# Fewer 64-slot experts, fewer of them fetched before the routing is known, and the embedding's weights fetched with them

## The chip, the core and the metric

The kernel runs on one core of a Trainium2 chip, in one launch. The metric is the time of that launch on the device in microseconds (us). Five engines work beside each other: TensorE multiplies matrices, VectorE and ScalarE do elementwise work and move results out of the accumulators, GpSimd does a little, and SyncE only issues DMA transfers, in the order in which they stand in its program.

## The reference

Two layers of a decoder trunk on 256 tokens of width 1024, all in 32-bit floats. Each layer mixes tokens (two kinds of attention, gates, an output projection), normalises, and then runs a mixture of experts plus a small per-layer embedding, and normalises again. The change touches the second half of a layer:

```python
def hierarchical_moe(x, w_rg, b_rg, w_re, b_re, w_g, w_u, w_d):
    ...
    g_val, g_idx = lax.top_k(g_prob, 1)          # one of 4 groups
    ...
    e_val, e_idx = lax.top_k(e_prob, TOP_K_IN_GROUP)   # 2 of its 8 experts
    ...
    for g in range(N_GROUPS):
        hg = jax.nn.silu(jnp.einsum('nd,edf->nef', xt, w_g[g])) * jnp.einsum('nd,edf->nef', xt, w_u[g])
        y = y + jnp.einsum('nef,efd->nd', hg * comb[:, g, :, None].astype(hg.dtype), w_d[g])
    return y.reshape(B, S, D)
...
ple = jax.nn.sigmoid(x @ w_ple_gate[i]) * (p[i] @ w_ple[i])
x = layer_norm(ALPHA * x + ffn + ple, ln2_g[i], ln2_b[i])
```

So 256 tokens are spread over 32 experts, two experts for each token: 512 token places in all. Every expert has 3 MB of weights (gate, up and down, each 1024 by 256).

## The kernel before

**Weights and places.** All big weights come from HBM in blocks of 512 KB, one DMA each. An expert is six blocks: four for gate and up (j = 0 to 3) and two for down (j = 4, 5). SBUF holds an arena of 47 places (`Arena`, `places=47`); a place holds one block, or one tile of activations of that size. `Held` takes a place and `free` gives it back. A load takes the place that has been free longest, and its DMA waits until the last user of that place is done. Which load gets which place is fixed when the program is built.

**Slots and groups.** An expert computes on a fixed number of token slots. `NBIG` experts have 64 slots, the others 32. TensorE takes 128 rows at a time, so a group is either two experts with 64 slots (a **pair**, 12 blocks) or four experts with 32 (a **four**, 24 blocks). `groups` lists them (`npair` pairs, then fours) and `order` says in which order they run. In this text group 0 is the one that runs first. Inside a group the work on TensorE is cut in strips of 32 rows, so a pair and a four issue the same number of instructions of the same size.

**Fixed and ranked experts.** The first `NFIX` experts are experts 0, 1, 2, ... by number. Their weights need no routing, so they are fetched while the attention half still runs, as places come free (`for gi in range(len(groups))` ... `fetch(r, j)`). The other experts are ranked by how many tokens they got; the fullest take the remaining 64-slot ranks. Their numbers land in `ids`, SyncE reads each of them (`value_load`, line 1034) and only then issues that expert's six DMAs (line 1040).

**One turn of the loop over groups.** TensorE's order is written by hand (`manual_schedule`): `front(gi+1)` multiplies the gathered tokens by gate and up; `back(gi)` multiplies the hidden activations by down; then the tokens of group gi+2 are gathered with a one-hot matrix, the hidden activations of gi+1 are transposed, the outputs of gi are scattered back into the accumulators (`combine`), `embeds(gi)` may add a piece of the embedding, and the scatter matrix of gi+2 is made (`ways_of`). `front` frees its blocks two k-steps at a time, `back` frees its blocks at its end.

**Embedding.** It is cut in four quarters (`Embed(q)`): two blocks each, and one more for every two quarters. Quarter 0 is always fetched early. `nemb` says how many further quarters are fetched before the routing is known; the others are fetched when their turn comes. `e0`, `e1`, `early` and `lastat` say after which group a quarter's half (`run(t)`, one half of the tokens) is computed.

**A check for overflow.** After `front` of group 4 (`ifat=3`) all engines branch on whether an expert got more tokens than it has slots (line 1191). Only then `leftover` runs a slow loop over all experts.

**The end of a layer.** `wide(2, l)` and `wide(3, l)` load the second normalisation's scale and shift (line 382) on SyncE's queue, between the second and third of the last group's eight down blocks. In layer 0 the first weights of layer 1 follow.

Of the kernel before, what the change touches and what calls it, by code (L numbers as in the profile page):

```python
# [41 lines left out]
FAR = 1000.0  # L42


NFIX = 6
NBIG = 12


SEC = ["iq", "sq", "sk", "sv", "dq", "dk", "dv", "ga0", "ga1", "gb0", "gb1"]
# [30 lines left out]

@with_exitstack
def tile_hybrid_trunk(ctx: ExitStack, tc: tile.TileContext, x_in, xT_in, pT_in, pos_in, ws, wik, wrt, lnv,
                      brt, lamv, sublnv, out, places=47, t2b=4, young=4, gsb=1, hTb=1, silb=2, nring=5, early=(4, 5, 6), nahead=4, apart=8, npre=36, wA=1, wB=1, wC=1, wD=1, wE=3, inorder=2, e0=2, e1=2,  nearly_=0, peng_=1, ifat=3, im=0, df=0, dh=15, nol=0, diag=1, rpool='0000', lastemb=1, lastat=6, pre_if=(4,5), npair=6, fh=False, fg=0, order=(0,1,2,6,3,7,4,8,5,9,10), engs=None, nemb=1, nwarm=9, nfine=2, nah=4, o1=False, o2=False, o3=True, o4=True, order2=True, pa=2, pb=7, f1=True):
    nc = tc.nc
    V, A, G = nc.vector, nc.scalar, nc.gpsimd

# [20 lines left out]
    def in_turn():  # L107

        return tc.issue_after(PE.last.ins)
# [14 lines left out]
    def bank():  # L124
        return ps.tile([P, 512], F32, tag="mm", bufs=4, name=nm("mm"))
# [128 lines left out]
    def constants():  # L254
# [14 lines left out]
        G.iota(kbon, pattern=[[-1, NE]], base=NE - 1, channel_multiplier=0, allow_small_or_imprecise_dtypes=True)  # L269
        V.tensor_scalar(kbon[:, :NFIX], kbon[:, :NFIX], 1.0e6, None, op0=OP.add)  # L270
        G.iota(kid[:, 0:1], pattern=[[0, 1]], base=0, channel_multiplier=1, allow_small_or_imprecise_dtypes=True)
        V.tensor_scalar(kid[:, 1:2], kid[:, 0:1], float(NFIX), 1.0e6, op0=OP.is_lt, op1=OP.mult)
        V.tensor_tensor(kid[:, 1:2], kid[:, 1:2], kid[:, 0:1], op=OP.subtract)
# [179 lines left out]
    for l in range(DEPTH):  # L453
# [414 lines left out]
        def places_of(b, mask, cols):  # L868

            n = cols.stop - cols.start  # L870
            PE.matmul(b[:, 0:n], trib, mask[:, 0, :], start=True, stop=True)
            PE.matmul(b[:, n:2 * n], onesb, mask[:, 0, :], start=True, stop=False)
            PE.matmul(b[:, n:2 * n], trib, mask[:, 1, :], start=False, stop=True)
            V.scalar_tensor_tensor(posm[:, :, cols], mask, -FAR, b[:, :2 * n].rearrange("p (t e) -> p t e", t=TT),
                                   op0=OP.mult, op1=OP.add)


        groups = [[(r, 2, 64)] for r in range(0, 2 * npair, 2)]
        small = NBIG
        for r in range(2 * npair, NBIG):  # L880
            n = min(2, NE - small)
# [42 lines left out]
        def marks_of(gi):  # L924

            gs = wt([P, TT, P], F32, "gs", gsb)
            c = 0
            for r, n, w in groups[gi]:
                marked[0] = V.tensor_tensor(gs[:, :, c:c + n * w].rearrange("p t (e s) -> p t e s", e=n),
                                            iom[:, None, None, :w].to_broadcast([P, TT, n, w]),  # L930
                                            posm[:, :, r:r + n, None].to_broadcast([P, TT, n, w]), op=OP.is_equal)
                c += n * w
            return gs
# [17 lines left out]
        places = bank()  # L951
# [5 lines left out]
        with in_turn():  # L957
            places_of(places, mkf[:, :, :NFIX], slice(0, NFIX))
        gs = marks_of(0)
        with tc.issue_after(marked[0].ins):  # L960
# [24 lines left out]
            V.tensor_scalar(perm, iom[:NE, :NE], FAR, kcol[:, 2:3], op0=OP.add, op1=OP.is_equal)  # L985
            V.tensor_copy(cw[:, :, :NFIX], cbf[:, :, :NFIX])
        with in_turn():
# [8 lines left out]
        cmi = ids[:, NE:]  # L996
        V.tensor_scalar(ids[:, :NFIX], iom[0:1, :NFIX], FAR, None, op0=OP.add)
        V.tensor_copy(ids[:, NFIX:NE], b[0:1, 2 * NE + NFIX:3 * NE])
        over = cut(NE, rows=1)
        for c, n in (slice(0, NBIG), 64.0), (slice(NBIG, NE), 32.0):  # L1000
            V.tensor_scalar(over[:, c], b[0:1, 3 * NE + c.start:3 * NE + c.stop], n, None, op0=OP.subtract)
# [185 lines left out]
        def leftover(most):  # L1187
            def onward(cols, n):
                V.tensor_scalar(posm[:, :, cols], posm[:, :, cols], float(n), None, op0=OP.add)

            with tc.If(most > 0, preferred_fallthrough_block=False):
                onward(slice(0, NBIG), -64)
                onward(slice(NBIG, NE), -32)
                with tc.For_i(0, 2, 1):
                    with tc.For_i(0, NE, 1) as r:
                        rest(r)
                    onward(slice(0, NE), -P)
                onward(slice(0, NBIG), 64 + 2 * P)
                onward(slice(NBIG, NE), 32 + 2 * P)
# [138 lines left out]
```

## Time and profile before

| | us |
|---|---|
| median of 3 runs | 966.4 (963.85 to 969.9) |
| the profiled execution | 968.06 |
| its span, first to last instruction | 966.5 |
| TensorE busy | 911.4 (94% of the span) |
| VectorE busy | 427.8 (44%) |
| ScalarE busy | 347.7 (36%) |

The profile is of one execution. Each layer has two halves: attention and projections (about 0 to 220 us and 470 to 697 us) and experts (about 228 to 471 us and 704 to 953 us). HBM gave 278.70 MB over the span, 289 GB/s on average. "Busy" on TensorE says that a multiplication was in flight, not that the array was full.

### The profile page before, as it was taken

How to read it: one execution, taken by the hardware profiler on the slowest of the kernel's cores; microseconds unless marked ns; L12 is line 12 of the kernel's file. 1: busy time of each engine (PE TensorE's matmuls, PEld its weight loads, DVE VectorE, ACT ScalarE, POOL GpSimd, SP SyncE). 2: the span in 40 equal slices, each digit the busy share in tenths (PEclk: the TensorE clock that was granted, in tenths of full speed). 3: DMA queues.
4: the chain of work that ended last, by engine and by line, in shares of the span. 5: the costliest groups of instructions: out<-in, count | busy, mean ns of one | idle time of the engine just before them, and what ended most of it. 6: DMA issues, size and time to landing. Idle time of an engine off the chain costs nothing. (4 is left out here: it accounts for less than half of the span.)

```text
span 966.5 us, 15937 instructions
## 1 busy us (share of the span) xinstructions
PE 911.4 (94%) x5761; PEld 605.7 (63%) x5761; DVE 427.8 (44%) x1068; ACT 347.7 (36%) x704; POOL 33.3 (3%) x37
## 2 busy tenths in 40 slices
PE   8999999999998988999799999999999989888994
PEld 5877777785545466544488777787754646456441
DVE  6796566873121211122468864778622121211123
ACT  6557586522111111112346667765121111111120
POOL 0000000100000000000400000001000000000000
PEclk9999999999999999999999999999999999999998
DMA  8994335767899999795997243456869999979933
GB/s 298 408 417 161 125 110 179 261 244 284 320 360 415 388 417 376 310 416 234 397 418 306 88 131 131 139 196 235 305 215 372 378 409 415 399 299 408 370 144 145
DMA packets 79013, 280.86 MB, mean 291 GB/s; under 512 B 9160, under 2 KB 9928, under 8 KB 78928
## 3 DMA queue, kind: packets, MB, share of 16 engines
q1 hardware_dynamic: 78784, 279.78, 76.0%
q8 instruction: 47, 0.77, 0.3%
q14 instruction: 38, 0.31, 0.1%
q10 hardware_dynamic: 144, 0.00, 0.0%
HBM read 278.70 MB, written 1.05 MB: 289 GB/s over the span
## 5 line engine op out<-in xcount | busy, mean ns | idle before, releaser
L92 PE MATMUL acc<-a,a 128*128 128x512 f32 x1440 | 353.2, 399 | 2.1 <-ACT a L208 1.3
L92 PEld LDWEIGHTS acc<-a,a 128*128 128x128 f32 x1440 | 266.0, 189 | 65.1 <-issue 3.2
L92 PE MATMUL mm<-a,a 128*32 128x512 f32 (+5 forms) x1776 | 235.1, 537 | 0.0
L208 ACT ACTIVATE a<-a 128x512 fp32r<-128x512 f32 (+1 forms) x247 | 150.6, 631 | 99.9 <-PE acc L92 69.0
L209 DVE TENSOR_TENSOR a<-a,a 128x512 fp32r<-128x512 f32 (+1 forms) x239 | 161.0, 695 | 50.0 <-ACT a L208 48.6
L92 PEld LDWEIGHTS mm<-a,a 128*32 128x32 f32 (+3 forms) x1776 | 110.7, 132 | 101.4 <-issue 91.1
L92 PE MATMUL mm<-a,hT 128*32 128x512 f32 x704 | 92.2, 604 | 9.0 <-DMA a<-ws 5.0
L92 PEld LDWEIGHTS mm<-gs,a 128*128 128x128 f32 x704 | 80.4, 192 | 17.2 <-PE mm L92 11.7
L92 PE MATMUL mm<-gs,a 128*128 128x128 f32 x704 | 84.7, 278 | 0.0
L1050 ACT ACTIVATE sil<-mm 128x256 f32<-128x256 f32 x22 | 8.4, 383 | 183.2 <-PE mm L92 165.9
L92 PEld LDWEIGHTS mm<-a,hT 128*32 128x32 f32 x704 | 24.3, 111 | 71.5 <-issue 56.5
L1051 DVE SCALAR_TENSOR_TENSOR sil<-sil,wsl,mm 128x256 f32<-128x256 f32 x22 | 10.6, 481 | 131.4 <-ACT sil L1050 131.2
L209 DVE TENSOR_TENSOR t<-mm,t 128x512 fp32r<-128x512 f32 x44 | 30.4, 692 | 68.7 <-ACT t L208 68.7
L208 ACT ACTIVATE t<-mm 128x512 fp32r<-128x512 f32 x44 | 26.3, 597 | 79.0 <-PE mm L92 79.0
L763 DVE TENSOR_TENSOR sil<-sil,mm 128x256 f32<-128x256 f32 x16 | 6.7, 420 | 107.4 <-ACT sil L762 107.4
L92 PE MATMUL acc<-t,sT 128*128 128x512 f32 x176 | 48.8, 413 | 0.0
L906 ACT ACTIVATE a<-mm 128x512 f32<-128x512 f32 x40 | 23.9, 598 | 50.1 <-PE mm L92 50.1
L919 DVE CAST sT<-mm 128x256 fp32r<-128x256 f32 x22 | 9.3, 425 | 69.1 <-PE mm L92 69.1
L92 PEld LDWEIGHTS acc<-t,sT 128*128 128x128 f32 x176 | 31.4, 190 | 9.0 <-issue 2.5
L762 ACT ACTIVATE sil<-mm 128x256 f32<-128x256 f32 x16 | 6.1, 383 | 79.6 <-PE mm L92 79.6
L92 PE MATMUL acc<-t,identr 128*128 128x256 f32 x32 | 12.4, 388 | 21.8 <-ACT t L208 20.6
L548 ACT ACTIVATE t<-mm,mx 128x128 f32<-128x128 f32 (+1 forms) x64 | 26.0, 421 | 10.7 <-DVE mx L545 10.7
(197 smaller groups left out, 648.1 us busy)
## 6 DMA issues: line engine op xcount, KB each, us to landing
a<-ws SPq DMA_DIRECT2D x523, 512.0 KB, 8.4
a<-x_in SPq DMA_DIRECT2D x2, 512.0 KB
out<-a SPq DMA_DIRECT2D x4, 256.0 KB, 2.7
a<-xT_in SPq DMA_DIRECT2D x3, 256.0 KB
a<-wik SPq DMA_DIRECT2D x2, 288.0 KB, 7.6
a<-ws SPq DMA_DIRECT2D x2, 256.0 KB, 4.2
pT<-pT_in SPq DMA_DIRECT2D x2, 256.0 KB
a<-wrt SPq DMA_DIRECT2D x2, 144.0 KB, 2.8
```

Source lines behind the costliest of these rows:

```text
L92: self.last = nc.tensor.matmul(*a, **k)
L208: copied[0] = A.activation(hi, src, AF.Copy)
L209: copied[1] = eng.tensor_tensor(lo, src, hi, op=OP.subtract)
L548: A.activation(e[:, i * nk:(i + 1) * nk], b[:, i * nk:(i + 1) * nk], AF.Exp, bias=mx[:, i:i + 1], accum_out=sums[i])
L762: A.activation(g, b[:, :256], AF.Sigmoid)
L763: V.tensor_tensor(g, g, b[:, 256:], op=OP.mult)
L906: A.activation(xg, b.rearrange("p (k s) -> p k s", k=4), AF.Copy)
L919: V.tensor_copy(sT, b[:, :2 * P].rearrange("p (t q) -> p t q", t=TT))
L1050: A.activation(sil, gu[:, :FE], AF.Sigmoid)
L1051: V.scalar_tensor_tensor(sil, sil, wsl, gu[:, :FE], op0=OP.mult, op1=OP.mult)
```

## The change

```diff
-NFIX = 6
-NBIG = 12
+NFIX = 4
+NBIG = 8
...
-... early=(4, 5, 6) ... lastat=6 ... npair=6 ... order=(0,1,2,6,3,7,4,8,5,9,10) ... nemb=1 ...
+... early=(3, 4, 5) ... lastat=5 ... npair=4 ... order=(0,1,2,4,3,5,6,7,8,9) ... nemb=3 ...
```

Eight experts instead of twelve have 64 slots, and 24 instead of 20 have 32. Before there were six pairs and five fours; now there are four pairs and six fours, ten groups instead of eleven. In run order (P a pair, F a four) it was P P P F P F P F P F F and is now P P P F P F F F F F. Four experts instead of six are fetched before the routing is known (24 blocks instead of 36), and three quarters of the embedding instead of one (beside quarter 0): seven blocks instead of two. Quarters 1, 2 and 3 are computed after groups 3, 4 and 5 instead of 4, 5 and 6. All other settings stay, the 47 places too.

SyncE's queue in layer 0, where the fetches that need no routing end and the ranked ones begin (`a_...` is a place's tile, `ws` the weights, line 1040 an expert's block, line 164 an embedding's). Before:

```order
L1040 DMA a_2301<-ws 128x1024
L1040 DMA a_2303<-ws 128x1024
L1040 DMA a_2305<-ws 128x1024
L164 DMA a_2311<-ws 128x1024
L1034 TENSOR_LOAD ids_2224
L1034 ISA x2
L1040 ISA
L1040 DMA a_2661<-ws 128x1024
```

Now:

```order
L1040 DMA a_2283<-ws 128x1024
L164 DMA a_2287<-ws 128x1024
L164 DMA a_2289<-ws 128x1024
L164 DMA a_2291<-ws 128x1024
L164 DMA a_2293<-ws 128x1024
L164 DMA a_2295<-ws 128x1024
L164 DMA a_2297<-ws 128x1024
L1034 TENSOR_LOAD ids_2224
L1034 ISA x2
L1040 ISA
L1040 DMA a_2530<-ws 128x1024
```

The embedding's blocks now stand ahead of the first read of `ids`, and the expert blocks ahead of it are fewer.

TensorE in layer 0 after the branch, from the end of group 3's `combine` to the start of `front` of group 5 (`sT` scatters, `gs` gathers, `identr` is the identity, the last rows are `front`'s). Before:

```order
L92 MATMUL acc_2075<-t_603_3136,sT_2637 128x512
L95 MATMUL mm_3176<-identr,gs_3139 128x128 x2
L92 MATMUL mm_3176<-cw_2177,gs_3139 128x4 x2
L92 MATMUL mm_3258<-a_3199,a_3141 32x512
L92 MATMUL mm_3258<-a_3210,a_3141 32x512
```

Now:

```order
L92 MATMUL acc_2075<-t_608_3164,sT_2657 128x512
L92 MATMUL mm_3203<-a_2285,a_2069 128x256 x4
L92 MATMUL mm_3203<-a_2287,a_2070 128x256 x4
L92 MATMUL mm_3203<-a_2082,pT_1485 128x256 x2
L92 MATMUL acc_2072<-t_617_3217,identr 128x256 x2
L92 MATMUL mm_3222<-a_2285,a_2069 128x256 x4
L92 MATMUL mm_3222<-a_2287,a_2070 128x256 x4
L92 MATMUL mm_3222<-a_2082,pT_1485 128x256 x2
L92 MATMUL acc_2074<-t_620_3236,identr 128x256 x2
L95 MATMUL mm_3242<-identr,gs_3167 128x128 x2
L92 MATMUL mm_3242<-cw_2177,gs_3167 128x4 x2
L92 MATMUL mm_3324<-a_3265,a_3169 32x512
```

The embedding's quarter 1 (both halves of the tokens) has moved one group earlier, between `combine` of group 3 and `front` of group 5.

## Rows read from the trace of the kernel before

**Rows 1.** The page: busy time of each engine; TensorE and DMA in 40 slices.

```profile
PE 911.4 (94%) x5761; PEld 605.7 (63%) x5761; DVE 427.8 (44%) x1068; ACT 347.7 (36%) x704; POOL 33.3 (3%) x37
...
PE   8999999999998988999799999999999989888994
...
DMA  8994335767899999795997243456869999979933
```

**Rows 2.** Timeline of TensorE, one group of layer 0: start us, us, instructions.

```profile
261.38 7.07 PE L92 MATMUL mm<-a,a 128*32 128x512 f32 x64
268.27 3.62 PE L92 MATMUL mm<-a,hT 128*32 128x512 f32 x32
271.82 3.84 PE L92 MATMUL mm<-gs,a 128*128 128x128 f32 x32
...
275.63 2.10 PE L92 MATMUL acc<-t,sT 128*128 128x512 f32 x8
...
278.23 7.07 PE L92 MATMUL mm<-a,a 128*32 128x512 f32 x64
```

**Rows 3.** Waits on DMA, 228 to 470 us: us in total, times, longest.

```profile
PEld mm L92 <- DMA a<-ws: 8.7, 10, 2.3
...
PE mm L92 <- DMA a<-ws: 2.6, 5, 1.4
```

**Rows 4.** Timeline of TensorE, the last two groups of layer 0.

```profile
446.33 7.07 PE L92 MATMUL mm<-a,a 128*32 128x512 f32 x64
453.22 3.62 PE L92 MATMUL mm<-a,hT 128*32 128x512 f32 x32
...
464.12 1.05 PE L92 MATMUL mm<-a,hT 128*32 128x512 f32 x2 [1.41 <-DMA a<-ws]
...
468.04 2.76 PE L92 MATMUL mm<-a,hT 128*32 128x512 f32 x18 [0.24 <-DMA a<-ws]
```

**Rows 5.** The same, layer 1.

```profile
935.52 3.62 PE L92 MATMUL mm<-a,hT 128*32 128x512 f32 x32
...
952.89 2.22 PE L92 MATMUL acc<-t,sT 128*128 128x512 f32 x8
```

**Rows 6.** Timeline of SyncE's queue around the first ranked fetch, layer 0.

```profile
216.66 0.33 SPq L164 DMA_DIRECT2D a<-ws  x1
228.44 10.98 SPq L1040 DMA_DIRECT2D a<-ws  x9
```

**Rows 7.** The same, layer 1.

```profile
704.52 4.81 SPq L1040 DMA_DIRECT2D a<-ws  x5
```

**Rows 8.** Timeline of SyncE's queue at the end of layer 0.

```profile
436.61 2.88 SPq L1040 DMA_DIRECT2D a<-ws  x3
456.04 0.59 SPq L382 DMA_DIRECT2D a<-lnv  x2
456.85 3.07 SPq L1040 DMA_DIRECT2D a<-ws  x6
```

**Rows 9.** Line 1040's fetches, 228 to 460 us: count; time from issue to landing.

```profile
L1040 SPq DMA_DIRECT2D a<-ws x156: 332/333/1205, 228.4 to 459.6; - x156
...
DMA to landing us min/median/max: 3.3/8.4/10.9
```

**Rows 10.** Stretches: busy us (x) by engine, then granted clock, DMA share, GB/s.

```profile
244.00:248.00 4.00, 4.00 (x39) 1.59 (x41) 1.07 (x4) 0.60 (x1) 0.00 (x0) 1.00 0.29 73
384.00:392.00 8.00, 6.55 (x40) 2.73 (x43) 2.22 (x8) 0.80 (x2) 0.00 (x0) 0.79 0.38 126
400.00:440.00 40.00, 38.55 (x311) 21.86 (x309) 7.86 (x20) 6.76 (x14) 0.00 (x0) 1.00 1.03 416
448.00:457.00 9.00, 9.00 (x87) 2.70 (x79) 1.60 (x3) 0.99 (x3) 0.00 (x0) 1.00 0.02 8
900.00:920.00 20.00, 20.00 (x180) 9.84 (x176) 4.28 (x12) 3.43 (x7) 0.00 (x0) 1.00 0.99 395
```

**Rows 11.** Timeline of TensorE: one embedding quarter, first and following instructions.

```profile
343.90 3.61 PE L92 MATMUL mm<-a,a 128*128 128x256 f32 x16
...
356.98 0.38 PE L95 MATMUL mm<-identr,gs 128*128 128x128 f32 x2
```

**Rows 12.** Timeline of TensorE around the overflow branch of layer 0, and later.

```profile
316.03 5.34 PE L92 MATMUL mm<-a,hT 128*32 128x512 f32 x32 [2.09 <-DVEq L1191]
...
327.71 7.07 PE L92 MATMUL mm<-a,a 128*32 128x512 f32 x64
...
387.56 8.77 PE L92 MATMUL mm<-a,a 128*32 128x512 f32 x64
```

More of the change, by code (lines that the diff above doesn't have):

```diff
@@ L82, in tile_hybrid_trunk @@
 def tile_hybrid_trunk(ctx: ExitStack, tc: tile.TileContext, x_in, xT_in, pT_in, pos_in, ws, wik, wrt, lnv,
-                      brt, lamv, sublnv, out, places=47, t2b=4, young=4, gsb=1, hTb=1, silb=2, nring=5, early=(4, 5, 6), nahead=4, apart=8, npre=36, wA=1, wB=1, wC=1, wD=1, wE=3, inorder=2, e0=2, e1=2,  nearly_=0, peng_=1, ifat=3, im=0, df=0, dh=15, nol=0, diag=1, rpool='0000', lastemb=1, lastat=6, pre_if=(4,5), npair=6, fh=False, fg=0, order=(0,1,2,6,3,7,4,8,5,9,10), engs=None, nemb=1, nwarm=9, nfine=2, nah=4, o1=False, o2=False, o3=True, o4=True, order2=True, pa=2, pb=7, f1=True):
+                      brt, lamv, sublnv, out, places=47, t2b=4, young=4, gsb=1, hTb=1, silb=2, nring=5, early=(3, 4, 5), nahead=4, apart=8, npre=36, wA=1, wB=1, wC=1, wD=1, wE=3, inorder=2, e0=2, e1=2,  nearly_=0, peng_=1, ifat=3, im=0, df=0, dh=15, nol=0, diag=1, rpool='0000', lastemb=1, lastat=5, pre_if=(4,5), npair=4, fh=False, fg=0, order=(0,1,2,4,3,5,6,7,8,9), engs=None, nemb=3, nwarm=9, nfine=2, nah=4, o1=False, o2=False, o3=True, o4=True, order2=True, pa=2, pb=7, f1=True):
     nc = tc.nc
```

## The prediction

> **What bounds the kernel now.** The page comes first. TensorE is busy for 94% of the span, and in the slices of the expert halves TensorE and DMA both read 9 [rows 1], so the page alone can't say which of them sets the pace there. The timeline of TensorE can. In the expert half it is a clockwork: `front` of a group starts at 261.38 and that of the next at 278.23, a period of 16.85 us, with no wait written in between [rows 2]. The waits view agrees: from 228 to 470 us TensorE and its weight loader waited for weight blocks 11.3 us in all [rows 3], and the timeline of the layer's end shows where, namely in `back` of the last group, whose blocks land one after another until 468.04 [rows 4]. The queue's own timeline says why. SyncE issued nothing between 439.5 and 456.04, when the two loads of line 382 at last got their places; six blocks stood behind them [rows 8]. Over 448 to 457 us DMA moved 8 GB/s, against 416 over 400 to 440 us [rows 10]. So TensorE sets the pace of the expert half up to the last group, DMA is kept a limited distance ahead by the 47 places, and a tail follows that the queue sets: 470.80 less 456.84, the end of the next-to-last group's `back`, or 14.0 us [rows 4], and 13.75 in layer 1 (952.89 less 939.14) [rows 5].
>
> **The change part by part.** *One group less.* A pair and a four have the same instructions, so what goes is one period: 16.85 us in each layer, 33.7 in all, as long as TensorE remains the bound. VectorE and ScalarE lose the same group's work; they were at 44% and 36% [rows 1] and give nothing further.
>
> *The embedding* keeps its instructions. One quarter takes TensorE 13.08 us (356.98 less 343.90) [rows 11] wherever it stands. That it runs one group earlier costs nothing by itself, but it decides when places come free (below).
>
> *Fewer blocks ahead of the routing.* Before, 156 expert blocks [rows 9] and five of the embedding's quarters 2 and 3 came behind the first read of `ids`; now 168 expert blocks do and none of the embedding's. A block takes 1.26 us of the queue (524,288 bytes at 416 GB/s [rows 10]), so seven more are 8.8 us more to move in each layer after 228.44, when the first ranked fetch is issued [rows 6]. The queue stood idle ahead of that moment already (its last fetch was issued at 216.66) and will be idle longer, at no cost. What covers the 8.8 us is that TensorE was the bound; whether the cover holds has to be counted.
>
> *Places.* When the numbers are known, 47 places hold 24 fixed blocks, 10 of the embedding, 4 of x and its transpose and 1 of gathered tokens; 8 are free. (Before it was 36, 5, 4, 1: one free. The queue then waited for TensorE to free more, the stretch at 73 GB/s from 244 to 248 us [rows 10]; that stop goes.) Up to the end of `back` of group 3, TensorE frees 48 blocks by the fronts of groups 0 to 4, 20 by the backs of groups 0 to 3 and 2 of the embedding's quarter 0. So 78 blocks can be issued up to 321.4 us, when that `back` ends (316.03 plus 5.34 [rows 12]). At 1.26 us each, 3.3 us after the first issue [rows 9] and with two short stops of 1 us, the 78th lands at about 331. Then the queue stops: quarter 1 now stands ahead of `front` of group 5, which begins not at 327.71 [rows 12] but 13.1 later. Quarter 1's own three blocks come free at about 336, the front's from 342.5 on, and a new block lands 3.3 us after its issue. That is a stop of some 7 us and one of 3, and one of 1 ahead of group 6. My estimate of all stops is 13 us. The bounds are 0 (no place is ever short) and 16: what the queue lost in the same stretch before, 155 blocks issued between 228.44 and 439.5 where 195 us would do. I take 13, near the upper one, because the stretches at 73 and 126 GB/s [rows 10] show that such stops are real.
>
> *Five fours in a row.* A four needs 24 blocks, 30.2 us of the queue, against TensorE's 16.85 us; a pair needs 15.1. In the last five groups TensorE catches up with the queue. The block that decides is number 160, the last one of `back` of group 8, the next-to-last group; the two loads of line 382 and the last six blocks are issued only after it, as before, so the tail stays at 14 us. In layer 0 it lands at 228.44 + 3.3 + 159 x 1.26 + 13 = 445.1, and the 18 instructions behind it take 2.8 us [rows 4], so this `back` ends at 447.9. TensorE alone would end it at 456.84 less 16.85 = 440.0. The later one counts: 447.9 instead of 456.84, a gain of 8.9 us, with 7.9 us of the removed period lost to a new wait for weights. In layer 1 the count starts at 704.52 [rows 7] and gives 923.9; TensorE alone would give 939.14 less 16.85 = 922.3 [rows 5]. The gain is 15.2. Layer 1 does better because it computes the last half quarter of the embedding (6.5 us) inside the loop and not after it, which gives the queue that much more time.
>
> *The clock.* After the 2.09 us wait at the overflow branch, 32 instructions took 5.34 us instead of 3.62 [rows 2, 12], and once later 64 took 8.77 instead of 7.07; the granted clock of 384 to 392 us was 0.79 [rows 10], a mixture of the two levels, 2.4 and 1.2 GHz. Such a fall costs 1.7 us. The new waits could add one in each layer; while TensorE waits for blocks a slower array costs nothing, so the bounds are 0 and 3.4 us for both layers, and I take 0.
>
> The sum is 8.9 + 15.2 = 24.1 us. From the profiled execution's 968.06 us this gives 944.0; that execution was 1.7 us above the median, so against 966.4 it is 942.3. I predict **942 us**.
>
> **The rivals.** *TensorE remains the bound throughout.* If the stops are short (5 us or less in layer 0, 11 in layer 1), both layers keep the whole 16.85: 966.4 less 33.7 = 932.7 us. For it: TensorE waited for nothing before the last group. Against it: the count above.
>
> *The queue is slower than I take it.* The bound would be the same, with a larger price of a block. The lowest rate in a stretch in which DMA was nearly full (0.99) is 395 GB/s [rows 10], 1.327 us for a block; 159 blocks are then 10.7 us later in each layer and the gain shrinks to 24.1 less 21.4, that is 964 us. Halfway, at 405 GB/s, it is 953, which I take for this case. For it: the rows differ by 5%. Against it: the 395 holds moments in which places were short. The Trainium skill ("DMA: Bandwidth & Descriptors", Specifications) speaks against the change more strongly: it puts what HBM gives one core at about 358 GB/s, by which a block would take 1.46 us and the whole, an estimate from that figure, would be near 1,000 us. This trace disagrees, with 416 GB/s over 40 us.
>
> *Stops as long as before, now where they count.* The queue is strictly in order, and places are assigned when the program is built; one block whose place is freed late holds up all behind it. Before, layer 0's queue lost 16 us up to 439.5 and 16.5 more at line 382 [rows 8], and TensorE hardly noticed, because it came later than the blocks. If a stop of the second kind falls ahead of block 160 now, the stops are 33 us instead of 13: both layers end 20 us later than forecast, which makes 24.1 us gained into 15.9 lost, 982 us. The change turns into a loss from about 25 us of stops on average (22 in layer 0, 28 in layer 1). For it: each of the last five groups asks for twice the blocks of a pair. Against it: the two loads of line 382 still stand behind block 162.
>
> *The change doesn't do what it says.* With 32 slots for 24 experts a crowded one would overflow, and `leftover` would stream all experts again: at least 64 x 6 blocks x 1.26 = 484 us in a layer. The reference's routing of its own inputs gives at most 23 tokens (layer 0) and 28 (layer 1) to an expert with 32 slots and at most 45 to one with 64. That ten groups are built, the program's order shows.
>
> **How the numbers follow.** Forecast 0.61; TensorE as the bound 0.12; a slower queue 0.17; longer stops 0.09; overflow 0.01. About 1%, or 9.7 us, is what a measurement of this kernel can tell from no change. Faster by more than that are the forecast, the first rival and 0.12 of the second: 0.85. Within 1% is the rest of the second, 0.05; slower are the last two, 0.10. The range runs from the first rival's 932 to 955: it holds the forecast (stops of 16 us give 948, one fall of the clock in each layer 3.4 more), the first rival and about half of the second, together 0.81.
>
> **What would show it.** In the profile of the changed kernel: ten `front` rows in each layer with a period of 16.85 us up to group 8 where no embedding stands between; stretches of low GB/s near 331 to 341 us; TensorE waiting for blocks in `front` of group 9 and above all `back` of group 8, some 8 us in layer 0 and under 2 in layer 1; then 14 us from that `back` to the end of the experts; the end of layer 1's experts moved from 953 to about 929 us. I am wrong if `front` of groups 5 to 8 waits for blocks, if the last blocks arrive well after 458 us in layer 0, or if the attention halves change length.

## The result, and the profile after

The changed kernel takes **956.0 us** (median of 4 runs, 953.3 to 957.7) against 968.2 for the kernel before beside it (963.9 to 969.9): a ratio of 0.988, 95% interval 0.984 to 0.992. It is faster by 12 us, half of the 24.1 us forecast, and outside the range of 932 to 955. The profiled execution is the lowest of the four (953.29 us, span 950.9).

The page of the changed kernel, against [rows 1]: 288 instructions of TensorE are gone, the work of two groups, yet its busy time has fallen by only 18.3 us where two periods are 33.7, and it still reads 94%; so the page hides that TensorE now waits more. DMA has a dip at slice 15.

```profile
PE 893.1 (94%) x5473; PEld 588.8 (62%) x5473; DVE 420.5 (44%) x1056; ACT 341.6 (36%) x692; POOL 33.4 (4%) x37
...
PE   8999999999998898999899999999999988988994
...
DMA  8995344755999969999999234356659998899993
```

Timeline of TensorE in the changed kernel, layer 0, against [rows 4, 12]: start us, us, instructions.

```profile
228.07 3.64 PE L92 MATMUL mm<-a,t 128*32 128x512 f32 x32 [0.16 <-ACT t L906]
...
316.47 5.34 PE L92 MATMUL mm<-a,hT 128*32 128x512 f32 x32 [2.09 <-DVEq L1191]
...
327.50 3.61 PE L92 MATMUL mm<-a,a 128*128 128x256 f32 x16
...
341.32 8.62 PE L92 MATMUL mm<-a,a 128*32 128x512 f32 x64
...
396.19 7.07 PE L92 MATMUL mm<-a,a 128*32 128x512 f32 x64
...
413.04 7.07 PE L92 MATMUL mm<-a,a 128*32 128x512 f32 x64
...
429.89 5.46 PE L92 MATMUL mm<-a,a 128*32 128x512 f32 x38
...
444.16 1.04 PE L92 MATMUL mm<-a,hT 128*32 128x512 f32 x2 [0.20 <-DMA a<-ws]
...
450.46 2.76 PE L92 MATMUL mm<-a,hT 128*32 128x512 f32 x18 [0.23 <-DMA a<-ws]
...
459.96 5.19 PE L92 MATMUL mm<-a,hT 128*32 128x512 f32 x8 [2.24 <-DMA a<-ws]
465.68 2.76 PE L92 MATMUL mm<-a,hT 128*32 128x512 f32 x18 [0.53 <-DMA a<-ws]
```

The order of events is the one forecast: quarter 1 at 327.50, `front` of group 5 at 341.32, the clockwork of 16.85 us from 396.19 on, and from the middle of `front` of group 9 (429.89) on mostly two instructions at a time, each pair waiting for a block. `front` of groups 5 to 8 waits for none. `back` of group 8 ends at 450.46 + 2.76 = 453.2 instead of the 447.9 forecast. The waits from 228 to 470 us, against [rows 3], have grown from 11.3 to 28.0 us:

```profile
PEld mm L92 <- DMA a<-ws: 23.2, 23, 3.1
...
PE mm L92 <- DMA a<-ws: 4.8, 12, 2.2
```

The same in layer 1, against [rows 5]:

```profile
698.99 3.64 PE L92 MATMUL mm<-a,t 128*32 128x512 f32 x32 [0.16 <-ACT t L906]
...
920.81 2.76 PE L92 MATMUL mm<-a,hT 128*32 128x512 f32 x18 [0.20 <-DMA a<-ws]
...
937.21 2.21 PE L92 MATMUL acc<-t,sT 128*128 128x512 f32 x8
```

Stretches of the changed kernel, columns as in [rows 10] (busy us of TensorE, its weight loader, VectorE, ScalarE and GpSimd; then granted clock, DMA share, GB/s):

```profile
230.00:232.00 2.00, 2.00 (x19) 0.61 (x12) 0.00 (x0) 0.00 (x0) 0.00 (x0) 1.00 0.78 270
232.00:234.00 2.00, 2.00 (x20) 1.88 (x18) 0.00 (x0) 0.27 (x1) 0.00 (x0) 1.00 0.84 283
234.00:236.00 2.00, 1.68 (x17) 1.13 (x20) 1.11 (x6) 1.61 (x2) 0.00 (x0) 1.00 0.97 322
236.00:240.00 4.00, 3.09 (x31) 0.79 (x23) 1.22 (x5) 0.38 (x1) 0.00 (x0) 1.00 1.00 401
...
330.00:342.00 12.00, 9.10 (x44) 6.76 (x46) 2.25 (x7) 1.60 (x4) 0.00 (x0) 0.96 0.60 212
342.00:346.00 4.00, 4.00 (x32) 1.05 (x28) 0.82 (x4) 0.00 (x0) 0.00 (x0) 0.69 0.08 28
346.00:350.00 4.00, 4.00 (x44) 1.12 (x40) 0.00 (x0) 0.00 (x0) 0.00 (x0) 1.00 0.91 290
350.00:400.00 50.00, 45.65 (x326) 29.08 (x322) 9.85 (x26) 8.50 (x18) 0.00 (x0) 1.00 1.00 399
400.00:440.00 40.00, 39.45 (x310) 19.02 (x302) 6.96 (x20) 6.10 (x12) 0.00 (x0) 1.00 1.03 415
```

What SyncE's queue waited for in the changed kernel from 320 to 350 us (us in total, times, longest):

```profile
SPq L1040 <- PE mm L92: 22.8, 7, 10.4
```

The queue waited for TensorE to free places; one wait lasted 10.4 us. Line 1040's fetches from 228 to 335 us, and from 330 to 344 us (count, first and last issue):

```profile
L1040 SPq DMA_DIRECT2D a<-ws x78: 332/333/1258, 228.9 to 324.8; - x78
...
L1040 SPq DMA_DIRECT2D a<-ws x3: 332/333/333, 336.0 to 338.5; - x3
```

That is the stop which the prediction counted: 78 blocks are issued, and the 79th has to wait. At 416 GB/s, 330 to 350 us would have carried 8.3 MB and carried 3.8: 10.8 us lost there, and 2.0 more from 350 to 400 (399 GB/s).

How much the queue lost in all is read from the block that `back` of group 8 waits for last. The first ranked fetch is issued at 228.90; at the prediction's even rate, without any loss, block 160 lands at 228.90 + 3.3 + 159 x 1.26 = 432.5. TensorE starts behind it at 450.46. The queue's losses were **17.9 us** in layer 0 where 13 stood in the sum; in layer 1 (first issue 699.79) it is 920.81 less 903.4, **17.4 us**.

### The profile page after: what moved, and what is told of

Same layout as the page of the kernel before. It is cut to its first block, busy times and chain, and to the rows that moved or that the text cites. A ratio compares the mean times of both kernels' runs of the same rounds, so it can differ in the third digit from the quotient of the medians.

```text
span 950.9 us, 15376 instructions
## 1 busy us (share of the span) xinstructions
PE 893.1 (94%) x5473; PEld 588.8 (62%) x5473; DVE 420.5 (44%) x1056; ACT 341.6 (36%) x692; POOL 33.4 (4%) x37
## 5 line engine op out<-in xcount | busy, mean ns | idle before, releaser
L92 PE MATMUL mm<-a,a 128*32 128x512 f32 (+5 forms) x1648 | 225.5, 533 | 0.8 <-DMA a<-ws 0.8
L92 PEld LDWEIGHTS mm<-a,a 128*32 128x32 f32 (+3 forms) x1648 | 107.3, 134 | 97.7 <-issue 81.2
L92 PE MATMUL mm<-a,hT 128*32 128x512 f32 x640 | 97.4, 608 | 11.5 <-DMA a<-ws 7.2
L92 PEld LDWEIGHTS mm<-gs,a 128*128 128x128 f32 x640 | 73.1, 192 | 15.5 <-PE mm L92 10.1
L92 PE MATMUL mm<-gs,a 128*128 128x128 f32 x640 | 77.0, 278 | 0.0
L209 DVE TENSOR_TENSOR t<-mm,t 128x512 fp32r<-128x512 f32 x40 | 27.7, 692 | 79.0 <-ACT t L208 79.0
L208 ACT ACTIVATE t<-mm 128x512 fp32r<-128x512 f32 x40 | 23.9, 597 | 88.5 <-PE mm L92 88.5
L92 PE MATMUL acc<-t,sT 128*128 128x512 f32 x160 | 44.2, 411 | 0.0
L906 ACT ACTIVATE a<-mm 128x512 f32<-128x512 f32 x36 | 21.5, 597 | 45.1 <-PE mm L92 43.8
L92 PEld LDWEIGHTS acc<-t,sT 128*128 128x128 f32 x160 | 28.3, 189 | 8.5 <-issue 2.5
```

Of the source, the lines that this page charges most:

```text
L92: self.last = nc.tensor.matmul(*a, **k)
L208: copied[0] = A.activation(hi, src, AF.Copy)
L209: copied[1] = eng.tensor_tensor(lo, src, hi, op=OP.subtract)
L906: A.activation(xg, b.rearrange("p (k s) -> p k s", k=4), AF.Copy)
```

## The experiments

Four kernels ran on one chip and four on another, each beside the kernel before, which is why that one has two medians; the row "changed" is the result above, against 968.2. For all of them the same four stretches are read from the timeline of TensorE as above, in one profile each: from the layer's first expert matmul (228.07 and 698.99 in the changed kernel) to the end of `back` of the next-to-last group ("to back"), and from there to the end of the last group's `back` ("tail"). TensorE alone would need 16.85 less than the kernel before to `back`: 212.4 and 218.6.

| kernel | median us | ratio to before (95%) | layer 0: to back, tail | layer 1: to back, tail |
|---|---|---|---|---|
| before | 965.2 and 967.0 | | 229.2, 14.0 | 235.4, 13.8 |
| changed | 956.0 | 0.988 (0.984 to 0.992) | 225.2, 15.2 | 224.6, 13.7 |
| changed, again | 954.9 | 0.988 (0.985 to 0.992) | 225.3, 14.7 | 227.0, 13.6 |
| embedding later | 937.1 | 0.971 (0.968 to 0.974) | 212.8, 14.9 | 221.6, 13.6 |
| embedding on demand | 954.7 | 0.988 (0.985 to 0.992) | 225.1, 14.7 | 225.8, 13.4 |
| fewer blocks, changed | 934.5 | 0.967 (0.964 to 0.970) | 214.0, 14.2 | 218.5, 14.4 |
| fewer blocks, before | 966.2 | 0.999 (0.996 to 1.001) | 229.1, 15.1 | 235.6, 15.1 |
| embedding earlier, before | 968.2 | 1.001 (0.998 to 1.004) | 230.8, 14.0 | 233.8, 13.7 |
| fetch part alone | 968.1 | 0.999 (0.996 to 1.002) | 230.9, 15.0 | 235.4, 15.0 |
| embedding later, pair last | 932.9 | 0.963 (0.960 to 0.966) | 219.5, 9.1 | 217.4, 7.6 |

**The changed kernel again.** No edit.

> The changed kernel itself, once more, beside the three edits on the same chip. All theories: 953 to 958 us, 8 to 14 us below the kernel before. The theory of the stops says that layer 0 again loses its largest piece, about 11 us, at 334 to 345 us, and that back of group 8 ends near 453. If the missing time were variation of one run, this one would come out near 942, or its layer-0 back of group 8 near 448.

It took 954.9 us, and its layer 0 needed 225.3 us to `back` where the first execution needed 225.2. The missing half is no variation of one run.

**The embedding one group later.**

```diff
-... early=(3, 4, 5) ... lastat=5 ...
+... early=(4, 5, 6) ... lastat=6 ...
```

> The changed kernel with the embedding's quarters 1, 2 and 3 put back behind groups 4, 5 and 6 (lastat 6), all else as changed. Theory of the stops (quarter 1 ahead of front of group 5 keeps the queue without places for some 11 us): the stop at 334 to 345 us shrinks to a few us, back of group 8 in layer 0 ends near 441 to 444 instead of 453 and in layer 1 near 921 instead of 923.6; 942 to 947 us, 8 to 14 below the changed kernel. Theory of the places (seven embedding blocks fetched ahead hold places and make the stops): they hold them longer now, so the time is the same or some us worse, 955 to 960. Theory that the loss lies elsewhere (clock, run, attention half): within 2 us of the changed kernel.

937.1 us, 17.8 below the changed kernel on the same chip: more than the 8 to 14 that I expected, and decisive. Timeline of TensorE in this kernel, around `front` of group 5 and at the end of layer 0:

```profile
315.65 3.64 PE L92 MATMUL mm<-a,hT 128*32 128x512 f32 x32 [2.09 <-DVEq L1191]
325.63 7.07 PE L92 MATMUL mm<-a,a 128*32 128x512 f32 x64
...
429.08 7.07 PE L92 MATMUL mm<-a,a 128*32 128x512 f32 x64
435.97 4.12 PE L92 MATMUL mm<-a,hT 128*32 128x512 f32 x32
```

Stretches of this kernel, columns as above:

```profile
324.00:332.00 8.00, 8.00 (x71) 3.32 (x73) 1.37 (x6) 0.00 (x0) 0.00 (x0) 1.00 1.03 417
332.00:342.00 10.00, 10.00 (x83) 6.62 (x76) 2.29 (x4) 3.05 (x6) 0.00 (x0) 1.00 1.03 419
342.00:352.00 10.00, 8.55 (x39) 7.07 (x39) 0.85 (x2) 0.80 (x2) 0.00 (x0) 1.00 1.02 412
```

The waits of its queue from 320 to 350 us:

```profile
SPq L1040 <- PE mm L92: 3.5, 2, 3.3
```

The edit moves quarters 2 and 3 as well, but ahead of `front` of group 5 it takes away quarter 1 alone. `front` of group 5 runs 15.7 us earlier (0.8 of them because this expert half starts earlier, 1.7 because `back` of group 3 is not slow here) and frees its places while the queue needs them; the dip to 28 GB/s is gone, the longest wait for TensorE falls from 10.4 to 3.3 us, and `front` of group 9 and `back` of group 8 lose 0.5 us (4.12 for 3.62) where they lost 13. Layer 0 is bound by TensorE (212.8 against 212.4). Layer 1 gains 3.0 us against the first execution of the changed kernel and 5.4 against the second; the 3.0 us that it still lacks to TensorE alone fit the clock, with four slow rows of `front` and `back` (8.77 us three times, 4.79 once, for 7.07 and 3.62) where the kernel before has two. The theory that the loss lies elsewhere falls.

**Quarters 2 and 3 on demand.**

```diff
-... nemb=3 ...
+... nemb=1 ...
```

> The changed kernel with nemb=1: quarters 2 and 3 are again fetched when their turn comes, five blocks fewer ahead of the routing and five more behind it. Theory of the stops: the stop is ahead of front of group 5 with or without them, and it is as long or a little longer because more places are free at first and run out at the same point; back of group 8 moves by less than 3 us, the time stays within 4 us of the changed kernel. Theory of the places: five more places are free for experts, the stops shrink from 18 to about 12 us and the time falls by 6 to 8 us to about 948. Theory of a plain queue bound without stops: five blocks more behind the ids cost 6.3 us, 962.

954.7 us, as the theory of the stops expected, but not for its reason. `back` of group 8 now waits for its last block at 449.33; five more blocks stand ahead of it, so without losses it would land at 227.77 + 3.3 + 164 x 1.26 = 437.7. The losses fell to 11.6 us, as the theory of the places said (about 12), and the five blocks cost 6.3 us more of the queue. The two cancel here: the five blocks fetched ahead cost as much in stops as they cost in the queue when fetched on demand.

**Fewer blocks, in both kernels.** In every four but the last, the down blocks of the third and fourth expert are left out, and those of the first two are used in their place. TensorE's work stays; the queue gets 20 blocks less per layer in the changed kernel and 16 in the kernel before.

```diff
+            own = [r for r, _ in experts(gi)]
+            if js[0] == 4 and len(own) == 4 and gi < len(groups) - 1:
+                own = own[:2] * 2
...
-                for r, _ in experts(gi):
+                for r in own:
...
-            free(*wr[0], *wr[1])
+            free(*dict.fromkeys(wr[0] + wr[1]))
```

> The changed kernel, but in the fours except the last the down blocks of the third and fourth expert are not loaded; those of the first two are used in their place, so the output is not the reference's. TensorE's instructions are the same; the queue carries 20 blocks, 25 us, fewer in each layer. Theory that the queue with its stops is the whole loss against one removed period per layer: both layers become bound by TensorE, back of group 8 ends near 440 to 442 in layer 0 and near 920 in layer 1, and the time is 930 to 938. Theory that part of the loss is on TensorE or outside the expert half: at most 3 us better than the changed kernel, 951 or more.

> The kernel before, but in its fours except the last the down blocks of the third and fourth expert are not loaded and those of the first two are used in their place, so the output is not the reference's; TensorE's instructions are the same, the queue carries 16 blocks, 20 us, fewer in each layer. If TensorE sets the pace of the kernel before: no change, 962 to 970 us, back of the next-to-last group ends within 1 us of 456.8 in layer 0 (measured from the same start of the half). If the queue already sets the pace there (the rival: the loss was in the kernel before too, and the change only kept it), it falls by 10 us or more, below 956. The attention half of layer 1 is read beside it: the changed kernels have it 2.4 us shorter than the one profile of before; if that is variation of an execution, it may be short here too.

934.5 us in the changed kernel, 20.4 below it, with both layers within 1.7 us of TensorE alone; in the kernel before the ratio is 0.999 (0.996 to 1.001). So the queue sets the pace of the changed kernel and did not set that of the kernel before. With fewer blocks the changed kernel is 30.7 us below the kernel before on that chip, of the 33.7 that two periods are worth; the queue is nearly the whole of what the change failed to bring.

**The change's other parts alone, in the kernel before.**

```diff
-... early=(4, 5, 6) ... lastat=6 ...
+... early=(3, 4, 5) ... lastat=5 ...
```

> The kernel before with the embedding's quarters 1, 2 and 3 moved one group earlier (behind groups 3, 4 and 5, lastat 5), which is that part of the change alone. Theory: the queue loses about the same 10 us ahead of front of group 5, but TensorE comes later than the blocks in eleven groups, so the end of back of the next-to-last group does not move: 962 to 970 us. Rival (the earlier place itself costs TensorE, by the clock or by order, some 10 us whatever the queue does): 973 or more.

```diff
-NFIX = 6
+NFIX = 4
...
-... nemb=1 ...
+... nemb=3 ...
```

> The kernel before with four experts instead of six fetched before the routing and three quarters of the embedding instead of one, its eleven groups as they were: the fetching part of the change alone. Theory: the queue has slack against TensorE's eleven groups, so nothing moves: 962 to 970 us. If what is fetched ahead brought the gain (or takes back a part of it), the time is 956 or less (972 or more).

Neither moves the time: 1.001 (0.998 to 1.004) and 0.999 (0.996 to 1.002). With the embedding earlier the hole is there all the same. Stretches of that kernel:

```profile
330.00:342.00 12.00, 9.10 (x45) 6.26 (x47) 2.94 (x10) 1.60 (x4) 0.00 (x0) 0.95 0.66 248
342.00:346.00 4.00, 4.00 (x32) 1.17 (x28) 0.12 (x1) 0.00 (x0) 0.00 (x0) 0.73 0.26 88
346.00:350.00 4.00, 4.00 (x40) 1.17 (x36) 0.04 (x1) 0.38 (x1) 0.00 (x0) 1.00 0.86 250
```

By the same count, 9.6 us are lost there, and TensorE doesn't pay for them. The earlier embedding costs nothing among eleven groups and 12 us (layer 0) among ten.

**The fourth pair last as well.**

```diff
-... early=(3, 4, 5) ... lastat=5 ... order=(0,1,2,4,3,5,6,7,8,9) ...
+... early=(4, 5, 6) ... lastat=6 ... order=(0,1,2,4,5,6,7,8,9,3) ...
```

> The changed kernel with the embedding's quarters behind groups 4, 5 and 6 and, beside that, the fourth pair run last instead of fourth (order 0, 1, 2, 4, 5, 6, 7, 8, 9, 3: three pairs, six fours, a pair). A pair has four down blocks where a four has eight. If the tail behind the next-to-last back is set by the last group's down blocks that the queue has yet to issue, the tail shrinks from 15 us to about 10 in each layer, while six fours in a row cost some 2 us of waiting in layer 0: 927 to 934 us against 937. If the tail is set by something else (the loads of line 382, the last group's own work), it stays at 15 us and the time at 937 or above.

932.9 us, the fastest kernel of the study, 34 us below the kernel before. The tail shrinks as expected, to 9.1 and 7.6 us: it is set by the last group's down blocks. Layer 1 keeps the 6.0 us and is 4.2 shorter to `back` as well; its `front` and `back` have no slow row in this profile, where the kernel with the embedding later alone has four. Layer 0 keeps nothing: with the pair last, the block that `back` of group 8 waits for last is the 164th and no longer the 160th, so this `back` waits for blocks again, and with three slow rows the way to its end is 219.5 us instead of 212.8. And some 5 us more are lost at the start of layer 1. Timeline of GpSimd in this kernel:

```profile
463.99 1.25 POOL L209 TENSOR_TENSOR a<-a,a 128x512 fp32r<-128x512 f32 x1 [10.81 <-DMA a<-ws]
465.21 0.58 POOL L405 TENSOR_TENSOR rs<-rs,few 128x1 f32<-128x1 f32 x1
```

Timeline of its VectorE:

```profile
465.83 3.43 DVE L414 SCALAR_TENSOR_TENSOR a<-a,rs,a 128x512 f32<-128x512 f32 x2 [2.47 <-POOL rs L405]
```

Timeline of its TensorE:

```profile
446.91 2.76 PE L92 MATMUL mm<-a,hT 128*32 128x512 f32 x18 [0.19 <-DMA a<-ws]
...
467.64 1.12 PE L95 MATMUL mm<-identr,a 128*128 128x128 f32 x4 [3.46 <-DVE a L414]
```

The first of these TensorE rows is the end of `back` of group 8. GpSimd waits for a weight block of layer 1 and holds the normalisation's line 405 behind it; VectorE waits for that, TensorE for VectorE. From the end of layer 0's last `back` to layer 1's first expert matmul it takes 235.4 us instead of 230.5 in the kernel with the embedding later alone. Of these 4.9 us the rows show some 3: TensorE's wait ahead of line 95 is 3.46 us here and 0.51 there. That part is the queue's debt, which has moved on to the next layer's weights; the rest was not followed up.

## Why the prediction was wrong

**The step that failed** is the term "My estimate of all stops is 13 us", with its bounds of 0 to 16. Measured are 17.9 and 17.4 us, and 18.0 and 19.8 in the second profile of the changed kernel. Ahead of `back` of group 8 every microsecond of it goes into the time, in both layers, so a miss of 5 us became one of nearly 10. The mechanism was right: places run out after 78 blocks, and the queue stops until quarter 1 is done. Of the prediction's own signs of being wrong, `front` of groups 5 to 8 waited for nothing, but the last blocks of layer 0 came well after 458 us (the last wait ends at 465.68). Piece by piece, layer 0, where the landings of single blocks are taken from the trace:

- *The start of the fetches, not counted.* The sum let block n land at 3.3 + (n - 1) x 1.26 us, as if the queue ran at full rate from the first block. In the changed kernel it ran at 270 to 322 GB/s from 230 to 236 us; its fifth block landed at 239.81, 2.6 us later than that count. It was to be read ahead of the result: the kernel before has 254 to 320 GB/s in the same stretch (the rows below), and I took 3.3 us, the shortest landing of [rows 9], for a start in which blocks overlap.
- *Two short stops of 1 us*: 2.5 us; block 69 landed at 323.01, 5.1 us later than the count.
- *The stop ahead of `front` of group 5, "some 7 us and one of 3"*: 10.8 us by the stretches. Right in place, cause and nearly in size; that quarter 1 makes it, the embedding one group later shows. In layer 1 it is the largest piece too, 8.9 us: block 78 lands 6.1 us later than the count, block 86 15.0.
- *One of 1 ahead of group 6*: 2.0 us from 350 to 400.

Stretches of the kernel before:

```profile
230.00:232.00 2.00, 2.00 (x19) 0.93 (x12) 0.00 (x0) 0.00 (x0) 0.00 (x0) 1.00 0.82 254
232.00:234.00 2.00, 1.81 (x16) 1.58 (x14) 0.15 (x1) 0.69 (x2) 0.00 (x0) 1.00 0.89 320
234.00:236.00 2.00, 1.87 (x18) 1.11 (x22) 1.38 (x7) 1.19 (x1) 0.00 (x0) 1.00 0.98 293
```

The bound of 16 came out too small for a like reason. It compares times of issue, while the sum counts landings, and a block that is issued deep in the stream takes longer than 3.3 us to land. The 150th block of the kernel before (the embedding's five are counted, as in the prediction's 155), issued at 432.85:

```profile
L1040 SPq DMA_DIRECT2D a<-ws x1: 333/333/333, 432.9 to 432.9; - x1
...
DMA to landing us min/median/max: 9.9/9.9/9.9
```

It landed at 442.74, where the sum's own count gives 228.44 + 3.3 + 149 x 1.26 = 419.5. By landings the kernel before had lost 23.3 us and not 16, and all four measured values lie inside such a bound.

**TensorE as the bound of the kernel before**: right, shown by the unchanged time with 16 blocks fewer per layer. **One group less is worth 16.85 us per layer as long as TensorE binds**: right; with the embedding later, layer 0 comes to 212.8 us against 212.4. **The seven more blocks, covered as long as TensorE was the bound**: right, the fetch part alone moves nothing. **The fall of the clock, taken at 0**: right in the profiled execution; it has two slow rows of `front` and `back` in each layer, as the kernel before (in layer 0 the 5.34 us of `back` of group 3 and the 8.62 us of `front` of group 5, with a granted clock of 0.69 from 342 to 346 us). The changed kernel's second profile has three such rows in layer 0 and the same time to `back`, 225.3 us; in layer 1 it has four and takes 2.4 us more.

**The tail stays at 14 us**: 13.7 in layer 1; 15.2 in layer 0, 1.3 more than before, a small second miss. Whether the change makes it is open: two variants of the kernel before have 15.0 and 15.1 there.

With these sizes the sum closes. Layer 0: 8.9 forecast, less 4.9 (stops) and 1.3 (tail), gives 2.7; measured from the first expert matmul to the end of the last `back`, 243.2 less 240.4, 2.8. Layer 1: 15.2 less 4.4 gives 10.8; measured 249.2 less 238.3, 10.9. Since the loss is read from that block's lateness, the closing says only that nothing else took part; that the pieces of layer 0 add up to 17.9 is the better check. The two spans differ by 15.6 us; the 1.9 beyond 13.7 comes from the attention half of layer 1, 232.9 us before and 230.6 after. That is not the change: variants of the kernel before show both (230.3 with fewer blocks, 230.4 with the fetch part alone, 232.3 with the embedding earlier). The profiled execution is also the fastest of its four. In the second profile (955.1 us, nearer the median) the halves gain 3.2 and 8.6 us, together near the 12 us of the medians.

**The rivals.** TensorE as the bound throughout (932.7) needed stops of 5 us or less in layer 0, and that was about the right condition: with the embedding later, block 158 lands 5.6 us later than the count, and the kernel takes 937. A slower queue is refuted: 415 GB/s from 400 to 440 us [rows 10: 416]. There the prediction cited the Trainium skill's 358 GB/s as what one core gets. The Trainium skill's "HBM Reference" ("Specifications (TRN2)") also says that a core streaming alone measures about 425; this trace, with 415 and 416 GB/s over 40 us on one core, is near that figure and not near 358. A stop at line 382 ahead of block 160, or an overflow, did not occur. The bounds should have been made from the landings of the kernel before, start included, and not from its issues.

## What to carry to other kernels

Work taken from the engine that sets the pace is worth its time only up to the next resource. A run with less of that resource's traffic shows whether it is the bound (0.999 in the kernel before, 20.4 us in the changed one), but not how near it is while it isn't; that is read from how late its transfers land against an even rate. A stop of an in-order queue costs nothing while the consumer comes later than the blocks, and its whole length once the consumer waits for them, so an order tuned under the old bound (here, one group's place for the embedding, 17.8 us) has to be set again with the change. Fetching ahead into a fixed number of places need not gain anything: five blocks moved from behind the routing to ahead of it changed nothing here.

## What the runs showed of the hardware

After an idle stretch the queue did not begin at its full rate: 270, 283 and 322 GB/s in three stretches of 2 us from 230 to 236 us and 401 from 236 to 240, against 415 from 400 to 440, which is 2.0 to 2.6 us on the landings of the changed kernel and of the one with the embedding later. What holds the queue back there, no run shows. The attention half of layer 1 took 230.3 to 232.9 us in the profiles of this study, the fastest kernel left out, without a link to what was edited. In the one profile of before, VectorE's line 414 took 3.45 us there instead of 2.87 and two of TensorE's first instructions of layer 1 took 1.14 us instead of 0.71, with a granted clock of 0.87 from 477 to 490 us; why executions differ there stays open.
